# Moving one gate tanh and one weight split ahead of other ScalarE work, at the end of the token mixer's block loop

## The chip, the cores and the metric

The kernel runs on one core of one Trainium2 chip. The metric is the device time of one execution in microseconds (us), the median of several runs.

## The reference

The program is one layer of a hybrid backbone over 512 latent tokens of 1024 channels, with 256 context tokens as a prefix. The part that matters here is the end of the token mixer:

```python
glu_l, xr_l, gt_l, mg_l = jnp.split(hl @ w_in, SPLIT_IN, axis=-1)
...
y_a = _conformer_conv(glu, dw_conv, ln_conv_g, ln_conv_b, w_proj_conv)
y_b = (rec.astype(gt.dtype) * jax.nn.gelu(gt)) @ w_proj_lru
g_a, g_b = jnp.split(mg, 2, axis=-1)
return (jax.nn.sigmoid(g_a) * y_a + jax.nn.sigmoid(g_b) * y_b) @ w_out
```

`_conformer_conv` is a depthwise convolution of width 31 over the tokens, then a LayerNorm over the channels, a swish and a projection. After the mixer come a residual, a gated feed-forward part with a 3x3 depthwise convolution, and another residual; they are untouched here.

## The kernel before, in words

Channels lie on partitions, in eight blocks of 128, and tokens along the free axis. Every large product is float32 made of three fp32r matmuls (`mm3`, L133 to L136): each operand is kept as a high part and a low part, and high x high, high x low and low x high are summed in PSUM. A block of 128 output channels over 512 tokens takes 8 x 3 = 24 matmuls (`block`, L142).

Weights come in blocks of 512 KB through one list, in the order of use. `dma_to` (L97) issues the load of a block into a ring of three `raw` buffers from the SP queue. `cvt_to` (L108) splits it: ScalarE (ACT) rounds it into `whi` (L122), and GpSimd (POOL) subtracts that from the raw block into `wlo` (L123); both go to rings of four buffers. `W(key, look=2)` (L127) splits everything up to two blocks past the one asked for. At the place of the change the list is ga 0, ga 1, gb 0, gb 1, yb 0, gb 2, yb 1, gb 3, yb 2 and so on (L200 to L206): ga and gb are the columns of `w_in` for the two gates, yb those of `w_proj_lru`.

The schedule is written out by hand: each engine runs its instructions in the order of the code, and the tile framework adds the semaphore waits. The stretch concerned does this, in the order of the code:

- The block loop ends with the last scan (L655 to L658 on VectorE, DVE) and eight gelus (L674 on ACT).
- TensorE (PE) computes ga 0 and ga 1 (`ga_mm`, L775) into PSUM, while `gt_post` (L677) makes the input of the yb products: eight multiplications of gelu and scan on DVE (L679), eight roundings on ACT (L139, `rgh`), and eight subtractions (L140, `rgl`), six on DVE and those of blocks 2 and 5 on POOL.
- `ga_act` (L780) takes the tanh of a finished ga block from PSUM into the tile `sa` (L781). `sa` is a new tile in the space of the gelu buffers `ge` of the last blocks, so its first write comes after the last reads of those.
- `offload` (L559) does taps of the 31-wide convolution for channel blocks 6 and 7 on ACT (L565), and adds them up on POOL (L567).
- The loop at L793 runs over b = -1 to 7. It computes gb b+1 on PE, takes its tanh (`gate_act`, L384, tile `tg`), computes yb b, and joins both on DVE (`gate_mul`, L388). In between, `fill(n)` (L573) puts n instructions of the convolution on DVE (`conv31`, L525; L541).

PSUM for these products is two one-bank and two two-bank buffers, handed out by turns (`mm_any`, L80). ga 0, gb 0 and yb 0 follow one another on the two-bank pair, so yb 0 takes the buffer of ga 0, and yb 1 that of gb 0. ga 1, gb 1 and gb 2 follow on the one-bank pair, so gb 2 takes the buffer of ga 1.

When the convolution is through (`fill(1000)`, L830), POOL adds its last two blocks into `lnsum` (L553), and PE sums that over the channels into `mean` (L832). PE does these two matmuls between the two halves of ga 3; DVE then goes on with the LayerNorm (L839).

Of the kernel before, what the change touches and what calls it, by code (L numbers as in the profile page):

```python
# [37 lines left out]
def backbone_kernel(es: ExitStack, tc: tile.TileContext, x, ctxt, par, wadq, wada, win, wgate, wpc, wpl, wout,  # L38
# [20 lines left out]
    def col(name, i=0, n=None):  # L59
        o, w = _OFF[name]  # L60
        return P[:, o + i:o + (w if n is None else i + n)]
# [7 lines left out]
    def flat(t):  # L69
        return t.rearrange("p a b -> p (a b)") if len(t.shape) == 3 else t  # L70
# [9 lines left out]
    def mm_any(name):  # L80
        turn[0] += 1
        return mm1(name) if turn[0] % 2 else mm2(name)[:, 0:512]
# [8 lines left out]
    seq, index, raws, ready, pos = [], {}, {}, {}, {"dma": 0, "cvt": 0}  # L91
# [5 lines left out]
    def dma_to(i):  # L97
        while pos["dma"] < min(len(seq), i + 1):
            n = pos["dma"]
            src, shape = seq[n][:2]  # L100
            if n < 5:
                raws[n] = pq.tile([128] + shape, F32, tag="wa", bufs=10, name="raw")
            else:
                raws[n] = ring.tile([128] + shape, F32, tag="raw", bufs=3, name="raw")
            nc.sync.dma_start(out=raws[n], in_=src)
            pos["dma"] += 1

    def cvt_to(i):  # L108
        while pos["cvt"] < min(len(seq), i + 1):
            n = pos["cvt"]  # L110
            dma_to(n)
            _, shape, dst, raw, eng = seq[n]
            if raw:
                ready[n] = raws.pop(n)
            else:
                if dst is None:
                    hl = (ring.tile([128] + shape, F32R, tag="whi", bufs=4, name="whi"),
                          ring.tile([128] + shape, F32R, tag="wlo", bufs=4, name="wlo"))
                else:
                    hl = dst()  # L120
                t = raws.pop(n)
                S.activation(out=flat(hl[0]), in_=flat(t), func=AF.Copy)  # L122
                eng.tensor_sub(flat(hl[1]), flat(t), flat(hl[0]))  # L123
                ready[n] = hl
            pos["cvt"] += 1

    def W(key, look=2, ahead=2):  # L127
        i = index[key]
        cvt_to(i + look)
        dma_to(i + look + ahead)  # L130
        return ready[i]
# [10 lines left out]
    def block(ps, w, rh, rl, ks=range(NB)):  # L142
        hi, lo = w
        for k in ks:
            mm3(ps, hi[:, k, :], lo[:, k, :], rh[:, k, :], rl[:, k, :], k == 0, k == NB - 1)
# [236 lines left out]
    def gate_act(ps):  # L382
        t = t_tile("tg")
        S.activation(out=t, in_=ps, func=AF.Tanh, scale=0.5)  # L384
        return t

    def gate_mul(t, ps, dst):
        V.scalar_tensor_tensor(out=dst, in0=t, scalar=1.0, in1=ps, op0=ALU.add, op1=ALU.mult)  # L388
# [170 lines left out]
    def offload(n):  # L559
        for _ in range(min(n, 2 * n_off - off["k"])):  # L560
            k, b = 30 - off["k"] // 2, 6 + off["k"] % 2
            sc = col("dw31", 31 * b + k, 1)
            a = off["acc"][:, 512 * b - 3072:512 * b - 2560]
            o = a if k == 30 else off["prod"][:, 512 * b - 3072:512 * b - 2560]
            S.activation(out=o, in_=glu[:, b, k:k + T], func=AF.Copy, scale=sc)  # L565
            if k != 30:
                G.tensor_add(a, a, o)  # L567
            off["k"] += 1
# [4 lines left out]
    def fill(n):  # L573
        for _ in range(n):
            if not next(filler, False):
                return
# [100 lines left out]
    def gt_post(bs):  # L677
        for b in bs:
            V.tensor_mul(gts[b], gts[b], rec[:, b, :])  # L679
        for b in bs:  # L680
            split(gts[b], rgh[:, b, :], rgl[:, b, :], G if b % 3 == 2 else V)
# [98 lines left out]
    def ga_act(b):  # L780
        S.activation(out=sa[:, b, :], in_=gap[b][0], func=AF.Tanh, scale=0.5)  # L781
# [3 lines left out]
    ga_mm(1, look=1)  # L785
    cvt_to(index["gb", 1])
    gt_post(range(NB))
    cvt_to(index["yb", 0])
    yb = pd.tile([128, NB, T], F32, tag="d", name="yb")
    for b in (0, 1):  # L790
        ga_act(b)
    offload(4)
    for b in range(-1, NB):  # L793
        if b + 1 < NB:
            psg = mm_any("gb_ps")
            block(psg, W(("gb", b + 1)), Ahi, Alo)
            tn = gate_act(psg)
        if b < 0:
            t = tn
            continue  # L800
        fill(8 if b else 20)
        offload(2)
        ps = mm_any("yb_ps")
        block(ps, W(("yb", b)), rgh, rgl)
        gate_mul(t, ps, yb[:, b, :])
        t = tn
        fill(7)
        offload(2)
# [450 lines left out]
```

## Time and profile before

| what | value |
|---|---|
| median of 3 runs | 866.53 us (866.37 to 867.76) |
| profiled execution, its own time | 866.8 us |
| its span from first to last instruction | 865.0 us |
| PE busy | 848.0 us, 98% |
| DVE busy | 659.8 us, 76% |
| ACT busy | 431.5 us, 50% |
| POOL busy | 411.6 us, 48% |
| mean granted clock of PE | 0.998 of full speed |

A row of the timeline gives the start in us from the span's start, the length in us, the engine, the source line, the operation, the tile written and the tiles read; xN is a number of instructions merged into one row. In brackets at its end stands how long the engine was idle before it, and what ended that wait. Neighbouring instructions of an engine overlap a little, so a start can lie just ahead of the end of the one before.

### The profile page before, as it was taken

Reading aid. Unit: us, or ns where it says so; the run is one execution under the profiler, and the core shown is the slowest. Engines: PE = TensorE matmul, PEld = TensorE weight load, DVE = VectorE, ACT = ScalarE, POOL = GpSimd, SP = SyncE. Lnnn points to the kernel's source line nnn. Section 1 sums busy time; section 2 is a strip of 40 time slices with the busy share of each in tenths; the row PEclk is TensorE's granted clock in tenths of the full one; section 3 lists DMA queues with packets and bytes.
Section 4 is the critical chain, followed back from the end, with each engine's and each line's share of the span. In section 5 each row is a group of like instructions: output and inputs, shape, how many; then the busy total and the mean of one; then the engine's idle time right before and its main releaser. Section 6 shows DMA issues by size and latency. Waiting matters only on the chain.

```text
span 865.0 us, 11373 instructions
## 1 busy us (share of the span) xinstructions
PE 848.0 (98%) x4312; PEld 688.6 (80%) x4312; DVE 659.8 (76%) x932; ACT 431.5 (50%) x612; POOL 411.6 (48%) x227
## 2 busy tenths in 40 slices
PE   7999999999999999999999999999999999999997
PEld 6777888888877778877788889888888888888785
DVE  5355799999979999984555245999998989889204
ACT  5273777778777432226653255443443444345222
POOL 1234555566555565455332223355564456457820
PEclk9999999999999999999999999999999999999999
DMA  9952222222223232334843402314333333324402
GB/s 348 392 216 86 62 74 86 85 62 85 84 75 96 75 122 85 110 146 152 311 147 109 184 24 74 110 65 143 118 114 109 122 122 110 120 88 136 156 0 98
DMA packets 31398, 106.01 MB, mean 123 GB/s; under 512 B 3440, under 2 KB 3568, under 8 KB 31344
## 3 DMA queue, kind: packets, MB, share of 16 engines
q1 hardware_dynamic: 31344, 105.29, 35.0%
q8 instruction: 34, 0.56, 0.3%
q14 instruction: 20, 0.16, 0.1%
HBM read 103.17 MB, written 2.10 MB: 122 GB/s over the span
## 4 chain that ended last, share of the span: by engine, by line
PE 88%; DVE 6%; ACT 3%; issue 1%; DMA 1%; POOL 0%; SPq 0%; DVEq 0%; ACTq 0%; POOLq 0%
PE up_ps L135 9%; PE up_ps L134 9%; PE up_ps L136 9%; PE xr_ps L135 3%; PE xr_ps L136 3%; PE xr_ps L134 2%; PE ya_ps L134 2%; PE y_ps L134 2%; PE y_ps L135 2%; PE ya_ps L135 2%; PE ya_ps L136 2%; PE y_ps L136 2%; PE yb_ps L136 2%; PE yb_ps L135 2%; PE yb_ps L134 2%; PE g_ps L136 1%
## 5 line engine op out<-in xcount | busy, mean ns | idle before, releaser
L123 POOL TENSOR_TENSOR wlo<-raw,whi 128x1024 fp32r<-128x1024 f32 x117 | 290.0, 2491 | 223.1 <-ACT whi L122 216.7
L1053 DVE SCALAR_TENSOR_TENSOR cv<-zall,P,cv 128x512 f32<-128x512 f32 x240 | 161.8, 743 | 0.2
L541 DVE SCALAR_TENSOR_TENSOR cv<-glu,P,cv 128x512 f32<-128x512 f32 x228 | 153.2, 740 | 0.0
L122 ACT ACTIVATE whi<-raw 128x1024 fp32r<-128x1024 f32 x121 | 125.2, 1053 | 23.4 <-issue 11.0
L135 PE MATMUL up_ps<-Alo,whi 128*128 128x512 f32 (+1 forms) x352 | 132.7, 377 | 0.0
L134 PE MATMUL up_ps<-Ahi,whi 128*128 128x512 f32 (+1 forms) x352 | 132.0, 375 | 0.0
L136 PE MATMUL up_ps<-Ahi,wlo 128*128 128x512 f32 (+1 forms) x352 | 131.1, 372 | 0.0
L134 PEld LDWEIGHTS up_ps<-Ahi,whi 128*128 128x128 f32 x352 | 66.1, 188 | 13.7
L136 PEld LDWEIGHTS up_ps<-Ahi,wlo 128*128 128x128 f32 x352 | 66.2, 188 | 13.1
L135 PEld LDWEIGHTS up_ps<-Alo,whi 128*128 128x128 f32 x352 | 66.2, 188 | 12.6
L1039 POOL TENSOR_TENSOR acl<-fo,ach 128x512 fp32r<-128x512 f32 x20 | 26.0, 1300 | 85.6 <-ACT ach L1036 85.6
L1053 DVE SCALAR_TENSOR_TENSOR cv<-zall,P,cc 128x512 f32<-128x512 f32 x40 | 41.5, 1066 | 23.4 <-ACT cc L1027 23.4
L1025 ACT ACTIVATE zall<-up_ps 128x512 f32<-128x512 f32 x40 | 23.7, 593 | 63.4 <-PE up_ps L136 63.4
L1036 ACT ACTIVATE ach<-fo 128x512 fp32r<-128x512 f32 x20 | 12.7, 633 | 67.3 <-DVE fo L1035 67.3
L618 ACT ACTIVATE gate_ps<-gate_ps,P 128x768 f32<-128x768 f32 x32 | 28.0, 875 | 34.5 <-PE gate_ps L136 34.0
L384 ACT ACTIVATE tg<-gb_ps 128x512 f32<-128x512 f32 x8 | 4.8, 596 | 48.2 <-PE gb_ps L136 48.2
L1027 ACT ACTIVATE cc<-up_ps,P 128x512 f32<-128x512 f32 x40 | 27.3, 682 | 2.1 <-DVE cv L1053 2.1
L140 POOL TENSOR_TENSOR xl<-xc,xh 128x768 fp32r<-128x768 f32 x8 | 14.9, 1860 | 27.3 <-ACT xh L139 27.3
L1053 DVE SCALAR_TENSOR_TENSOR fo<-zall,P,cv 128x512 f32<-128x512 f32 x40 | 27.8, 734 | 0.0
L134 PE MATMUL yb_ps<-rgh,whi 128*128 128x512 f32 x64 | 25.4, 396 | 1.7 <-ACT sa L781 1.7
L136 PE MATMUL gb_ps<-Ahi,wlo 128*128 128x512 f32 x64 | 25.3, 395 | 1.0 <-POOL wlo L123 1.0
L134 PE MATMUL ga_ps<-Ahi,whi 128*128 128x512 f32 x64 | 26.0, 406 | 0.0
(387 smaller groups left out, 2114.7 us busy)
## 6 DMA issues: line engine op xcount, KB each, us to landing
raw<-in_win_dram SPq DMA_DIRECT2D x48, 512.0 KB, 3.3
raw<-in_wup_dram SPq DMA_DIRECT2D x40, 512.0 KB, 3.4
wa<-in_wada_dram SPq DMA_DIRECT2D x24, 512.0 KB, 6.0
raw<-in_wdn_dram SPq DMA_DIRECT2D x22, 512.0 KB, 3.3
wa<-in_wadq_dram SPq DMA_DIRECT2D x16, 512.0 KB, 9.2
raw<-in_wpl_dram SPq DMA_DIRECT2D x8, 512.0 KB, 3.3
raw<-in_wpc_dram SPq DMA_DIRECT2D x8, 512.0 KB, 5.0
raw<-in_wout_dram SPq DMA_DIRECT2D x8, 512.0 KB, 3.3
```

What stands on the lines that cost most here:

```text
L122: S.activation(out=flat(hl[0]), in_=flat(t), func=AF.Copy)
L123: eng.tensor_sub(flat(hl[1]), flat(t), flat(hl[0]))
L134: PE.matmul(o, lh, rh, start=first, stop=False)
L135: PE.matmul(o, lh, rl, start=False, stop=False)
L136: PE.matmul(o, ll, rh, start=False, stop=last)
L140: (eng or V).tensor_sub(lo, src, hi)
L541: V.scalar_tensor_tensor(out=cv[b] if k else glu[:, b, 0:T], in0=glu[:, b, k:k + T], scalar=col("dw31", 31 * b + k, 1), in1=cv[b], op0=ALU ...
L618: S.activation(out=lru[b, d, q], in_=lru[b, d, q], func=AF.Tanh, scale=0.5, bias=hb[:, i:i + 1])
L1025: S.activation(out=z[:, 1:1 + GH, 1:1 + GW], in_=ps.rearrange("p (r c) -> p r c", c=GW), func=AF.Copy)
L1027: S.activation(out=c, in_=ps.rearrange("p (r c) -> p r c", c=GW), func=AF.Copy, scale=col("dw9", 9 * (i + FW * (1 - s)) + 4, 1))
L1039: G.tensor_sub(acl[:, i, :], fo[i, 0], ach[:, i, :])
L1053: V.scalar_tensor_tensor(out=o, in0=zz[i, s][:, k // 3:k // 3 + GH, k % 3:k % 3 + GW], scalar=col("dw9", 9 * (i + FW * (1 - s)) + k, 1), i ...
```

## The change

```diff
     gt_post(range(NB))
-    cvt_to(index["yb", 0])
+    cvt_to(index["gb", 2])
     yb = pd.tile([128, NB, T], F32, tag="d", name="yb")
-    for b in (0, 1):
-        ga_act(b)
-    offload(4)
     for b in range(-1, NB):
         if b + 1 < NB:
             psg = mm_any("gb_ps")
...
             tn = gate_act(psg)
         if b < 0:
             t = tn
+            ga_act(0)
+            ga_act(1)
+            offload(4)
             continue
```

Ahead of the loop one weight block more is split, that of gb 2. The two ga tanh and the four offloaded taps now stand behind the first gb tanh, inside the loop. No instruction is added or removed. The order on PE, DVE and the SP queue is the same as before.

On ACT the place is the stretch between the roundings of `gt_post` (the x8 row) and the second gb tanh. `whi` is a weight block's rounding: of the two in the third and fourth row, the first is that of yb 0 and the added one that of gb 2.

```order
 L122 ACTIVATE whi<-raw 128x1024 x2
 L139 ACTIVATE rgh<-ge 128x512 x8
-L122 ACTIVATE whi<-raw 128x1024
+L122 ACTIVATE whi<-raw 128x1024 x2
+L384 ACTIVATE tg<-gb_ps 128x512
 L781 ACTIVATE sa<-ga_ps 128x512 x2
 L565 ACTIVATE off_acc<-glu,P 128x512 x2
 L565 ACTIVATE off_prod<-glu,P 128x512 x2
-L384 ACTIVATE tg<-gb_ps 128x512
-L122 ACTIVATE whi<-raw 128x1024
 L384 ACTIVATE tg<-gb_ps 128x512
 L122 ACTIVATE whi<-raw 128x1024 x2
```

The rounding of gb 2 and the tanh of gb 0 moved ahead of the two ga tanh and the four taps; the tanh of gb 1 now follows the taps directly.

On POOL the place is from the subtractions of `gt_post` (L140) to the first addition of the LayerNorm's sum (L546).

```order
 L123 TENSOR_TENSOR wlo<-raw,whi 128x1024 x5
 L140 TENSOR_TENSOR rgl<-ge,rgh 128x512 x2
-L123 TENSOR_TENSOR wlo<-raw,whi 128x1024
+L123 TENSOR_TENSOR wlo<-raw,whi 128x1024 x2
 L567 TENSOR_TENSOR off_acc<-off_acc,off_prod 128x512 x2
-L123 TENSOR_TENSOR wlo<-raw,whi 128x1024
 L546 TENSOR_TENSOR lnsum<-glu 128x512
 L123 TENSOR_TENSOR wlo<-raw,whi 128x1024 x7
```

The subtraction of gb 2 moved from behind the two additions of the taps to ahead of them, right behind the subtraction of yb 0.

## Rows read from the trace of the kernel before

**Rows 1.** The page, busy time of each engine: us, share, instructions.

```profile
PE 848.0 (98%) x4312; PEld 688.6 (80%) x4312; DVE 659.8 (76%) x932; ACT 431.5 (50%) x612; POOL 411.6 (48%) x227
```

**Rows 2.** Waits of PE from 300 to 865 us: total, times, longest.

```profile
PE yb_ps L134 <- ACT sa L781: 1.7, 1, 1.7
PE gb_ps L136 <- POOL wlo L123: 1.0, 1, 1.0
```

**Rows 3.** Windows: length; PE, PEld, DVE, ACT, POOL busy; granted clock; DMA share; GB/s.

```profile
296.00:304.00 8.00, 6.30 (x28) 4.80 (x27) 8.00 (x12) 4.59 (x8) 2.54 (x3) 1.00 0.22 66
308.00:388.00 80.00, 80.00 (x345) 64.34 (x344) 78.38 (x120) 17.80 (x21) 41.09 (x22) 1.00 0.37 125
```

**Rows 4.** Timeline of PE, the matmuls around its two waits, around mean, and the last.

```profile
297.97 0.39 PE L136 MATMUL gb_ps<-Ahi,wlo 128*128 128x512 f32 x1
300.06 0.50 PE L134 MATMUL yb_ps<-rgh,whi 128*128 128x512 f32 x1 [1.70 <-ACT sa L781]
...
305.98 0.39 PE L135 MATMUL gb_ps<-Alo,whi 128*128 128x512 f32 x1
307.36 0.50 PE L136 MATMUL gb_ps<-Ahi,wlo 128*128 128x512 f32 x1 [0.99 <-POOL wlo L123]
...
387.99 0.39 PE L136 MATMUL ga_ps<-Ahi,wlo 128*128 128x512 f32 x1
388.22 1.02 PE L832 MATMUL mean<-lnsum,ones 128*128 128x512 f32 x2
...
858.67 0.40 PE L136 MATMUL d2b<-whi,acl 128*128 128x512 f32 x1
```

**Rows 5.** Timeline of ACT: rounding of yb 0, ga tanh, rounding of gb 2.

```profile
292.94 1.04 ACT L122 ACTIVATE whi<-raw 128x1024 fp32r<-128x1024 f32 x1
299.41 1.09 ACT L781 ACTIVATE sa<-ga_ps 128x512 f32<-128x512 f32 x2 [5.43 <-DVE rgl L140]
...
303.31 1.06 ACT L122 ACTIVATE whi<-raw 128x1024 fp32r<-128x1024 f32 x1
```

**Rows 6.** Timeline of DVE: the last multiplications and subtractions, the convolution, the LayerNorm's start.

```profile
284.76 2.89 DVE L679 TENSOR_TENSOR ge<-ge,rec 128x512 f32<-128x512 f32 x1
...
294.60 2.89 DVE L140 TENSOR_TENSOR rgl<-ge,rgh 128x512 fp32r<-128x512 f32 x1
...
298.62 0.68 DVE L140 TENSOR_TENSOR rgl<-ge,rgh 128x512 fp32r<-128x512 f32 x1
...
303.83 8.64 DVE L541 SCALAR_TENSOR_TENSOR cv<-glu,P,cv 128x512 f32<-128x512 f32 x13
...
389.28 2.48 DVE L839 SCALAR_TENSOR_TENSOR glu<-mean,glu 128x512 f32<-128x512 f32 x4 [2.90 <-PE mean L832]
```

**Rows 7.** Timeline of POOL: weight subtractions (second of a pair, yb 0, gb 2), the last sums.

```profile
284.24 2.86 POOL L123 TENSOR_TENSOR wlo<-raw,whi 128x1024 fp32r<-128x1024 f32 x1
...
294.06 2.89 POOL L123 TENSOR_TENSOR wlo<-raw,whi 128x1024 fp32r<-128x1024 f32 x1 [0.53 <-ACT whi L122]
...
304.91 2.39 POOL L123 TENSOR_TENSOR wlo<-raw,whi 128x1024 fp32r<-128x1024 f32 x1
...
385.27 2.46 POOL L553 TENSOR_TENSOR lnsum<-lnsum,glu 128x512 f32<-128x512 f32 x2 [7.62 <-DVE glu L541]
```

**Rows 8.** Timeline of the SP queue: the issue of gb 2's raw block.

```profile
284.31 0.33 SPq L105 DMA_DIRECT2D raw<-in_win_dram  x1
```

**Rows 9.** DMA issues by line: count, KB each, median us to landing.

```profile
raw<-in_win_dram SPq DMA_DIRECT2D x48, 512.0 KB, 3.3
```

**Rows 10.** Windows of the program's end, columns as in rows 3.

```profile
858.00:862.00 4.00, 1.07 (x5) 0.54 (x3) 2.14 (x4) 0.98 (x3) 0.00 (x0) 0.96 0.00 0
862.00:865.00 3.00, 0.00 (x0) 0.00 (x0) 0.03 (x1) 0.00 (x0) 0.00 (x0) 0.50 0.45 175
```

**Rows 11.** Windows of L353's first matmuls alone: length; PE, PEld busy; clock; DMA; GB/s.

```profile
3.00:4.50 1.50, 1.50 (x9) 1.50 (x9) 1.00 1.01 347
4.90:6.40 1.50, 1.50 (x15) 1.50 (x15) 1.00 0.99 360
```

## The prediction

> **What bounds the kernel now.** I began with the busy times on the page: PE is busy 98% of the span [rows 1], so the time can only move where PE waits, or is made to wait. The view of waits names two waits of PE after 300 us and none later up to its last matmul [rows 2]: 1.7 us ahead of yb 0, for a ga tanh on ACT, and 1.0 us inside gb 2, for a weight subtraction on POOL. From there on PE runs without a gap [rows 3], so whatever PE loses or wins here arrives whole at the end, unless another wait takes it up before.
>
> The candidate for that is DVE. Between 308 and 388 us it is busy 78.38 of 80 us [rows 3], and the rest is its wait of 2.90 us for mean, of which 1.6 us lie inside the window [rows 6]. So the convolution ends when DVE's own work ends, whatever PE does. POOL's last sums follow and end at 385.27 + 2.46 = 387.73 us, and PE starts mean at 388.22, right behind a ga matmul [rows 4, 7]. The slack is 0.49 us: PE can come no more than about 0.4 us earlier here, and every us that DVE loses beyond it is lost for good.
>
> The next question is what releases the two waits. The ga tanh had waited 5.43 us for DVE's last subtraction of `gt_post` [rows 5], which ends at 298.62 + 0.68 = 299.30 [rows 6]; the tanh starts at 299.41, and yb 0 at 300.06. So this wait is not made by ACT's order. The wait in gb 2 is: its rounding ran only at 303.31 and its subtraction at 304.91 to 307.30, against PE at 307.36 [rows 4, 5, 7].
>
> **The change part by part.**
>
> *The wait in gb 2 goes.* Its raw block is issued at 284.31 and takes 3.3 us to land [rows 8, 9]. Its rounding can follow that of yb 0 at about 293.9 (292.94 + 1.04) [rows 5], and its subtraction on POOL that of yb 0, at 296.9 (294.06 + 2.89) [rows 7]. Both are done some 7 us ahead of PE. At PE's pace of 0.233 us the matmul that started at 307.36 was due at 306.21, and its own length of 0.50 in place of 0.39 delays the next by 0.11 [rows 4]: the gain on PE is 1.15 + 0.11 = 1.26 us.
>
> *The tanh order costs nothing by itself.* The tanh of gb 0 reads a block done well before 297.97 + 0.39, and needs no `sa`. The ga tanh still wait for DVE's last subtraction. The tanh of gb 1 follows the taps directly, and is wanted only when PE reuses its buffer, after yb 0 and gb 2, more than 10 us later. SP and PE keep their orders.
>
> *The moved subtraction meets DVE's subtractions.* This is the term that decides. Before, POOL was free from 296.95 to 302.40 (5.46 us ahead of the taps' additions), while DVE did its last three subtractions; now POOL subtracts gb 2 there. What two such instructions do to each other is in the trace. A DVE subtraction that starts alone takes 0.68 us. One that starts while POOL subtracts a weight block takes 2.89, and ends 0.54 after POOL's: the one at 294.60 ends at 297.49, POOL's at 296.95 [rows 6, 7]. Where POOL has two weight subtractions in a row, DVE gets one instruction in between and is then held again: POOL's second at 284.24 takes 2.86 (2.39 alone), and the DVE multiplication started at 284.76 takes 2.89 and ends 0.55 after it. That is the pattern of the change: yb 0's subtraction holds DVE's third until 297.49, then gb 2's (296.9 to about 299.76) holds the fourth, from 297.42 to about 300.3. The cost to DVE is 2.89 - 0.68 = 2.21 us. No time comes back where gb 2's subtraction used to be: there DVE ran convolution steps, 13 in 8.64 us, undisturbed by POOL [rows 6, 7].
>
> So the last subtraction ends at 301.51, the ga tanh starts at 301.62, and yb 0 at 302.27. DVE, which has no idle time to give, carries the 2.21 us to the end of the convolution: POOL's last sums end at 389.94 and mean can start at 390.00 (0.06 after, like PE behind POOL in gb 2).
>
> *PE's idle time, and its clock.* Behind the last matmul ahead of yb 0 (297.97 + 0.39 = 298.36) PE now idles until 302.27, 3.9 us in place of 1.7. With 1.7 the granted clock stayed at 1.00 [rows 3]. The one other end of a busy stretch in the trace is the last: PE's final matmul ends at 858.67 + 0.40 = 859.07 [rows 4], and the granted clock is 0.96 on average over 858 to 862 and 0.50 after it [rows 10]. That makes 0.3 us at half clock before 862, so it fell near 861.7, after 2.6 us of idleness. 3.9 us is on the far side of that, so I take the fall as the likelier case. PE then starts yb 0 at 1.2 GHz. The price comes from the program's start, by the matmuls' pace (the clock column has no lower value there): 9 in 1.5 us before 4.5 us, 15 in 1.5 us from 4.9 [rows 11]. Started at 1.50, they took 3.0 to 3.4 us to reach the high pace. At half pace such a stretch loses 1.5 to 1.7 us; I take 1.6. The bounds are nothing (the clock stays, as at 1.7 us of idleness) and twice that (two such stretches, if the first counts for too little).
>
> The Trainium skill, in "TensorE: Matmul & The Clock Gate", section "What's actually happening", says that the low clock is the default and that activity releases it, so that idleness brings it back. By that rule the fall would come and the sum is the higher one below; if the wait of 1.7 us is the measure, it would not, and the sum is the lower one. The trace of before holds both behaviours, and no wait of 3.9 us between.
>
> **Sum.** PE's arrival at mean: + 2.21 (yb 0 later) - 1.26 (gb 2) + 1.6 (clock) = + 2.55 us, so 390.77; the sums were ready at 390.00, so nothing is added there. PE is gapless after it, hence + 2.55 at the end: 866.8 + 2.55 = 869.35 against the profiled execution. The median of the runs lies 0.27 below that execution, so the forecast is **869.1 us**.
>
> **The rivals.**
>
> *The clock stays up.* PE would reach mean at 388.22 + 0.95 = 389.17 and wait for the sums until 390.00, with a slower start of 0.11: + 1.89, or 868.4 us. For it: no wait of PE in the middle of this kernel has ever cost the clock. Against it: the tail fell after less.
>
> *DVE keeps its place, and the kernel is not slower.* If POOL's subtraction of gb 2 waits until DVE has done all six of its own, the splits end at 299.30 as before and only the gain at gb 2 is left. It decides at 297.4 us: whichever has started there, POOL's (due at 296.9) or DVE's fourth, holds the other. PE would then come to mean 1.26 us earlier, but the sums end at 387.73, so it starts at 387.79, with 0.11 for the restart: 0.32 us less, 866.2 us. For it: at 294.0 a DVE subtraction did get ahead, since POOL waited there for ACT until 294.06 [rows 7]. Against it: POOL's next instruction is ready here, its rounding being done at about 295, and the pair at 284.24 shows who wins then. The Trainium skill says the same in "SBUF — State Buffer", section "Who interferes with whom": a VectorE instruction with two SBUF inputs contends with a GpSimd one that reads SBUF, and the one issued first blocks the other. By that, this rival would need gb 2's rounding to be late.
>
> *Two stretches at half clock.* + 2.55 + 1.6 = + 4.15, or 870.7 us, if the first stretch holds too much idleness for the clock to come back.
>
> **How the numbers follow.** Forecast 0.52, clock stays up 0.30, DVE keeps its place 0.10, two stretches 0.08. The forecast's own spread is 868.5 to 869.4 (1.0 to 1.7 us for the clock, as the fall may come before PE starts again, and some 0.2 on the 2.21). With the case of the clock staying up, and the scatter of a median on both, the range is 867.5 to 869.9; it leaves out the two small cases. What a measurement of this kernel can tell from no change is about 0.2%, 1.7 us, so up to 868.3. The forecast lies above that nearly whole (0.49 of its 0.52), the case at 868.4 about half (0.15), the last case whole: slower 0.72. Faster needs 1.7 us off, and the sums cap every gain at 0.4: 0.03, for what I have not seen. The rest, 0.25, is the same.
>
> **What would show it.** In the profile after: gb 2's subtraction on POOL near 296.9; one more DVE subtraction of 2.9 us, and the last ending near 301.5; the ga tanh near 301.6; PE's wait ahead of yb 0 at 3.9 us in place of 1.7, and none in gb 2; a granted clock below 1.00 between 300 and 308, and the first matmuls of yb 0 about twice 0.233 us apart; POOL's last sums ending near 389.9. I am wrong if all DVE subtractions after 297 us take 0.68, or if a wait ahead of mean swallows more or less than I say; if the clock stays at 1.00 the 1.6 us go, and a wait of about 0.8 us ahead of mean takes the place of part of them.

## The result, and the profile after

The changed kernel takes 873.13 us (median of 5 runs, 871.75 to 874.52) against 866.53 for the kernel before. The medians lie 6.6 us apart; the ratio that comes with a 95% interval is 1.0069 (1.0056 to 1.0082), or 6.0 us. Either way the time is outside the range of 867.5 to 869.9. The sign was forecast, the size was not, and the loss does not sit where it was put. The profiled execution took 871.75 us, with a span of 870.0 us against 865.0; it is the shortest of the five, so its rows explain 5 us of the loss.

The waits of PE from 282 to 440 us (total, times, longest) look quite different from [rows 2]:

```profile
PE mean L832 <- POOL lnsum L553: 6.1, 1, 6.1
PE yb_ps L136 <- POOL wlo L123: 0.6, 1, 0.6
PE ada_cp L310 <- DMA wa<-in_wada_dram: 0.2, 1, 0.2
```

Both waits of before are gone, the one ahead of yb 0 included. One of 6.1 us has appeared ahead of mean, and a small one of 0.6 us in yb 1. PE's timeline at the two places (start, length; it answers to [rows 4]):

```profile
297.49 0.39 PE L136 MATMUL gb_ps<-Ahi,wlo 128*128 128x512 f32 x1
297.72 0.39 PE L134 MATMUL yb_ps<-rgh,whi 128*128 128x512 f32 x1
...
385.13 0.39 PE L136 MATMUL ga_ps<-Ahi,wlo 128*128 128x512 f32 x1
391.61 2.08 PE L832 MATMUL mean<-lnsum,ones 128*128 128x512 f32 x2 [6.08 <-POOL lnsum L553]
```

yb 0 follows gb 1 at PE's pace of 0.23 us, at 297.72. The ga tanh run only at 301.09, as ACT's timeline shows (it answers to [rows 5]; the first row holds the roundings of yb 0 and gb 2):

```profile
292.43 2.00 ACT L122 ACTIVATE whi<-raw 128x1024 fp32r<-128x1024 f32 x2
294.33 0.57 ACT L384 ACTIVATE tg<-gb_ps 128x512 f32<-128x512 f32 x1
301.09 1.09 ACT L781 ACTIVATE sa<-ga_ps 128x512 f32<-128x512 f32 x2 [6.19 <-DVE rgl L140]
```

So yb 0 no longer depends on them. DVE's timeline answers to [rows 6]; everything in this execution starts 0.5 us earlier than in the one before (the first subtraction at 291.78 in place of 292.29):

```profile
291.78 9.22 DVE L140 TENSOR_TENSOR rgl<-ge,rgh 128x512 fp32r<-128x512 f32 x6
...
347.42 3.55 DVE L533 SCALAR_TENSOR_TENSOR cv<-glu,P,off_acc 128x512 f32<-128x512 f32 x2
...
393.72 2.48 DVE L839 SCALAR_TENSOR_TENSOR glu<-mean,glu 128x512 f32<-128x512 f32 x4 [3.49 <-PE mean L832]
```

The six subtractions took 7.01 us together before and take 9.22 now: the hold of 2.21 us that was forecast (a hold, here and below, is the time by which an instruction of one of these two engines is longer while one of the other runs). But there is a second one. The two steps that start the convolution of blocks 6 and 7 (L533, the only ones that add `off_acc`, which lies in SBUF like their other input) took 1.41 us before, and take 3.55 now. The same stretch before, DVE and then POOL:

```profile
345.72 1.41 DVE L533 SCALAR_TENSOR_TENSOR cv<-glu,P,off_acc 128x512 f32<-128x512 f32 x2
```

```profile
348.03 2.40 POOL L123 TENSOR_TENSOR wlo<-raw,whi 128x1024 fp32r<-128x1024 f32 x1 [4.00 <-ACT whi L122]
```

There DVE was through when POOL's weight subtractions came. POOL's timeline after (it answers to [rows 7]; the first row holds yb 0 and gb 2):

```profile
293.55 5.69 POOL L123 TENSOR_TENSOR wlo<-raw,whi 128x1024 fp32r<-128x1024 f32 x2 [0.54 <-ACT whi L122]
...
345.18 5.24 POOL L123 TENSOR_TENSOR wlo<-raw,whi 128x1024 fp32r<-128x1024 f32 x2 [4.02 <-ACT whi L122]
...
389.12 2.43 POOL L553 TENSOR_TENSOR lnsum<-lnsum,glu 128x512 f32<-128x512 f32 x2 [14.33 <-DVE glu L541]
```

PE is ahead, so POOL's pair comes at 345.18 in place of 348.03; DVE is behind, so L533 comes at 347.42 in place of 345.72, and now they meet. POOL's last sums end at 389.12 + 2.43 = 391.55, 3.8 us later than before, or 4.3 with the 0.5 us of the earlier start: the two holds of 2.21 and 2.14. The windows around mean, columns as in [rows 3], show what the wait brings with it:

```profile
388.00:391.00 3.00, 0.00 (x0) 0.00 (x0) 2.23 (x4) 0.00 (x0) 1.80 (x2) 0.50 0.00 0
391.00:393.00 2.00, 1.39 (x3) 0.84 (x3) 0.00 (x0) 0.00 (x0) 2.00 (x2) 0.50 0.00 0
393.00:395.00 2.00, 2.00 (x6) 1.25 (x5) 1.28 (x3) 0.56 (x1) 2.00 (x2) 0.64 0.17 16
395.00:397.00 2.00, 2.00 (x11) 1.59 (x10) 1.90 (x5) 1.95 (x5) 1.28 (x2) 1.00 0.67 246
```

The granted clock falls to 0.50, the 1.2 GHz level, while PE waits, and is back at 1.00 only near 394.4 (0.64 over 393 to 395 makes 1.4 us at 0.50). From 391.6 to 394.4 PE works 2.8 us at half pace and loses 1.4. The sum for this execution: the sums 4.3 us later, less 0.4 of slack that they had, 1.4 for the clock, 0.2 for a later DMA wait of PE, less the earlier start of 0.5: 5.0 us, the difference of the spans.

### The profile page after: what moved, and what is told of

The parts are those of the page before. It is cut to its first block, busy times and chain, and to the rows that moved or that the text cites. A ratio compares the mean times of both kernels' runs of the same rounds, so it can differ in the third digit from the quotient of the medians.

```text
span 870.0 us, 11374 instructions
## 1 busy us (share of the span) xinstructions
PE 849.6 (98%) x4312; PEld 689.6 (79%) x4312; DVE 663.2 (76%) x932; ACT 431.4 (50%) x612; POOL 412.2 (47%) x227
## 4 chain that ended last, share of the span: by engine, by line
PE 76%; DVE 15%; DMA 3%; issue 2%; ACT 2%; POOL 1%; SPq 0%; DVEq 0%; POOLq 0%; ACTq 0%
DVE cv L541 9%; PE up_ps L135 9%; PE up_ps L134 9%; PE up_ps L136 9%; PE xr_ps L136 2%; PE xr_ps L135 2%; PE xr_ps L134 2%; PE ya_ps L134 2%; PE y_ps L134 2%; PE ya_ps L136 2%; PE ya_ps L135 2%; PE y_ps L135 2%; PE y_ps L136 2%; DMA raw<-in_win_dram 1%; PE g_ps L134 1%
## 5 line engine op out<-in xcount | busy, mean ns | idle before, releaser
L541 DVE SCALAR_TENSOR_TENSOR cv<-glu,P,cv 128x512 f32<-128x512 f32 x228 | 153.3, 742 | 0.0
L140 POOL TENSOR_TENSOR xl<-xc,xh 128x768 fp32r<-128x768 f32 x8 | 14.9, 1859 | 27.3 <-ACT xh L139 27.3
L136 PE MATMUL yb_ps<-rgh,wlo 128*128 128x512 f32 x64 | 25.4, 397 | 0.6 <-POOL wlo L123 0.6
L136 PE MATMUL gt_ps<-Ahi,wlo 128*128 128x512 f32 x64 | 25.4, 397 | 0.3 <-POOL wlo L123 0.3
L134 PE MATMUL ya_ps<-slh,whi 128*128 128x512 f32 x64 | 25.6, 400 | 0.0
```

The lines of the kernel that those rows point to most:

```text
L134: PE.matmul(o, lh, rh, start=first, stop=False)
L136: PE.matmul(o, ll, rh, start=False, stop=last)
L140: (eng or V).tensor_sub(lo, src, hi)
L541: V.scalar_tensor_tensor(out=cv[b] if k else glu[:, b, 0:T], in0=glu[:, b, k:k + T], scalar=col("dw31", 31 * b + k, 1), in1=cv[b], op0=ALU ...
```

## The experiments

From the profile after I formed **theory A**: moving the tanh of gb 0 ahead frees PE (3 us), the early split holds DVE, the shifted timing of POOL and DVE holds it again at L533, and PE, which waits for DVE's result at mean, can only turn its lead into idle time. **Theory D**: that idle time also costs the clock. Ratios are to runs of the kernel before on the same chip, with 95% intervals.

**The tanh order alone** (the split stays where it was):

```diff
-    cvt_to(index["gb", 2])
+    cvt_to(index["yb", 0])
```

> Only the two ga tanh and the four taps move behind the first gb tanh; the split of gb 2 stays where it was. Theory A (a PSUM buffer goes to the next tile in the order in which its readers release it, and the order of the tanh decides that): yb 0 takes the buffer of gb 0 and starts without a wait, about 1.9 us earlier than before; gb 2 then waits some 3 us for its own late weight split, so that PE goes on at about 307.4 us as before; no DVE subtraction after 297 us is held (0.68 us each); POOL's last sums end as before, at 387.7. Time 866.5 us if the clock holds through the wait of 3 us, up to 868.2 if it falls. Rival B (the buffers rotate, and yb 0 lost its wait through the earlier weight split): yb 0 still waits 1.7 us, nothing else changes, 866.5 us.

Measured: 868.82 us, ratio 1.0021 (1.0012 to 1.0031). PE has one wait from 282 to 440 us, and yb 0 follows gb 1 without a gap:

```profile
PE gb_ps L136 <- POOL wlo L123: 2.6, 1, 2.6
```

The six subtractions take 7.02 us, as before. The time is 0.6 us above the upper value expected. The clock falls after this wait of 2.6 us:

```profile
310.00:313.00 3.00, 3.00 (x9) 2.32 (x8) 3.00 (x6) 0.00 (x0) 3.00 (x2) 0.50 0.44 141
```

PE does 9 matmuls in these 3 us, where 13 are its pace. So the order of the tanh alone frees yb 0, which rival B denied, and the lead is lost in gb 2. Of the 2.3 us by which this trace's span is longer than before, 1.0 lies ahead of the change (the first subtraction of `gt_post` starts at 293.33 in place of 292.29); the other 1.3 come behind the wait, where the clock is low.

**The split alone** (the kernel before, with gb 2 split early):

```diff
-    cvt_to(index["yb", 0])
+    cvt_to(index["gb", 2])
```

> Only the weight split of gb 2 moves ahead of the ga tanh; tanh and taps stay where they were. Theory A: yb 0 takes the buffer of ga 0, as in the kernel before, and now waits 3.9 us for the ga tanh, which waits for a DVE subtraction that is held once, for 2.2 us; the second hold (of the convolution step that reads off_acc) does not come, since POOL's pair is about 1 us late there and not early; POOL's last sums end near 389.9; 868.4 us if the clock holds, 869.1 if it falls: the case that was predicted for the whole change. Rival B (the early split frees yb 0): no wait ahead of yb 0, and the time is that of the whole change, 872 to 874 us.

Measured: 869.93 us, ratio 1.0031 (1.0019 to 1.0043). PE's wait, the subtractions of DVE, and the window behind the wait:

```profile
PE yb_ps L134 <- ACT sa L781: 3.8, 1, 3.8
```

```profile
292.11 9.18 DVE L140 TENSOR_TENSOR rgl<-ge,rgh 128x512 fp32r<-128x512 f32 x6
```

```profile
302.00:304.00 2.00, 1.97 (x5) 1.58 (x6) 2.00 (x4) 2.00 (x4) 0.00 (x0) 0.50 0.11 45
```

One hold, a wait of 3.8 us at yb 0, half clock behind it, and L533 at 1.41 us: this is what the prediction described, at + 0.31% where it had worked out + 2.55 us, 0.29%. For this half of the change its mechanism was right; the median lies 0.8 us above the 869.1 of the expectation, and the profiled execution, 868.90, is the shortest of the five.

**DVE's work reordered, first attempt** (four convolution steps while POOL subtracts gb 2):

```diff
             split(gts[b], rgh[:, b, :], rgl[:, b, :], G if b % 3 == 2 else V)
+            if b == 3:
+                fill(4)
```

> The changed kernel, with four steps of the convolution put between DVE's third and fourth subtraction, where POOL now subtracts gb 2; DVE does the same work in another order. Theory A (DVE is held twice, once for each of two separate meetings with POOL): the first hold is gone (all subtractions after the third take 0.68 us), the convolution is level with the kernel before until 345 us, and there one of the two steps that read off_acc is still held for about 2.2 us by POOL's pair; POOL's last sums end near 389.9, PE waits for them some 4.5 to 5 us, and the time is 868.5 to 870.5 us. Rival C (one hold explains the loss, the rest is the clock): nothing is left of the loss, POOL's last sums end at 387.7 and the time is at or below 867 us.

Measured: 872.96 us, ratio 1.0071 (1.0059 to 1.0083): outside both expectations. Both holds are gone in its trace, and POOL's last sums end at 387.50. But the convolution now ends four steps earlier in the code, so these sums stand ahead of a weight subtraction of ga on POOL's queue, and PE waits for that:

```profile
PE ga_ps L136 <- POOL wlo L123: 5.9, 1, 5.9
```

It says nothing for or against the second hold, nor on rival C. It does show how a change in DVE's order reaches PE through POOL's.

**The same, with POOL's order kept**:

```diff
+            if b == 3:
+                fill(4)
...
-        fill(8 if b else 20)
+        fill(8 if b else 16)
```

> As the run with four steps put between DVE's third and fourth subtraction, but these four are taken from the 20 ahead of the first join, so that from there on DVE's and POOL's orders are those of the changed kernel (in the earlier run the convolution ended four steps early in the code, and POOL's last sums came ahead of a weight subtraction of ga 3, for which PE then waited 5.9 us). Theory A: the first hold is gone, and DVE is level with the kernel before when it comes to the two steps that read off_acc, within 0.1 us of POOL's pair; whichever of them POOL gets ahead of is held for about 2.2 us. If one is, POOL's last sums end near 389.9, PE waits 4 to 5 us, 868.5 to 870.5 us; if none is, they end near 387.7, PE waits 2.3 to 2.8 us, 866 to 868 us. Rival C (the first hold is the whole loss): no wait ahead of mean of over 1 us, 864.5 us or less.

Measured: 868.66 us (866.01 to 870.92), ratio 1.0006 (0.9991 to 1.0020). In its profiled execution neither hold occurs, and PE's wait at mean is 1.3 us:

```profile
302.58 1.89 DVE L140 TENSOR_TENSOR rgl<-ge,rgh 128x512 fp32r<-128x512 f32 x3
...
348.24 1.42 DVE L533 SCALAR_TENSOR_TENSOR cv<-glu,P,off_acc 128x512 f32<-128x512 f32 x2
```

Of its twelve runs five lie at 866.0 to 866.7, one at 867.9 and six at 869.4 to 870.9. The lower ones fit the case of no hold, level with the lowest runs of the kernel before on that chip (866.2 to 866.9). What the upper ones had was not seen, but for the profiled one of 869.44, which lost its time at the program's start (last section). I had worked out a wait of 2.3 to 2.8 us; it is shorter since PE also waited 1.0 us in yb 1. Rival C falls: the wait ahead of mean is there with neither hold, and no run came to 864.5.

**DVE ahead of both meetings.** Seven steps of the convolution go between DVE's second and third subtraction, where POOL subtracts yb 0 and gb 2:

```diff
-            split(gts[b], rgh[:, b, :], rgl[:, b, :], G if b % 3 == 2 else V)
+            S.activation(out=rgh[:, b, :], in_=gts[b], func=AF.Copy)
+        for b in (2, 5):
+            G.tensor_sub(rgl[:, b, :], gts[b], rgh[:, b, :])
+        cvt_to(index["gb", 2])
+        for b in (0, 1, 3, 4, 6, 7):
+            V.tensor_sub(rgl[:, b, :], gts[b], rgh[:, b, :])
+            if b == 1:
+                fill(7)
...
-        fill(8 if b else 20)
+        fill(8 if b else 13)
```

> The changed kernel, with seven steps of the convolution taken from the 20 ahead of the first join of the loop (13 are left there) and put between DVE's second and third subtraction, so that DVE does them while POOL subtracts yb 0 and gb 2; the roundings and POOL's subtractions are issued in the same order as in the changed kernel. Theory A (the change gives PE about 3 us, and DVE's meetings with POOL take them away): no DVE subtraction from the second on is held; DVE is about 2 us ahead of the kernel before, passes the two steps that read off_acc ahead of POOL's pair, and POOL's last sums end near 385.5; PE waits under 1 us for them, the clock holds; 863.2 to 864.6 us. Rival F (PE's lead would be lost later whatever DVE does): 866 us or more, with a wait of PE of over 2 us that is not the one ahead of mean.

Measured: 865.29 us, ratio 0.9982 (0.9969 to 0.9994). PE's wait for the sums is down to 0.4 us, with 0.3 us in yb 1 and 0.5 us for a DMA. Theory A holds in its main point and rival F falls: with the holds of 2.2 us gone, the same change gains. The time is 0.7 us above what theory A expected, and the next run's rows show one reason, a third and shorter hold. The seven steps were not tried in the kernel before; there yb 0 waits for DVE's last subtraction, which they would delay, so a gain from them alone is unlikely but not excluded by a run.

**The same, and all of ga 3 ahead of mean**:

```diff
-        ga_mm(b, range(NB if b < 3 else 4))
+        ga_mm(b)
...
-    ga_mm(3, range(4, NB))
```

> As the run before, and all 24 matmuls of ga 3 stand ahead of mean in place of 12, which gives PE 2.8 us more to do before it needs POOL's sums. Theory A: no wait ahead of mean, the clock holds; 863.0 to 864.2 us, at most 0.8 less than the run before. Rival G (PE runs out of work behind mean, since the LayerNorm's sums are ready only some 10 us after it): a wait ahead of var of up to 1.5 us, and no gain against the run before.

Measured: **864.38 us, ratio 0.9962 (0.9948 to 0.9977)**, 2.5 us better than the kernel before by the medians and the lowest median of the study, though its interval overlaps that of the run before. It is 0.2 us above the expectation. From 282 us to the end PE has one wait:

```profile
PE yb_ps L136 <- POOL wlo L123: 0.3, 1, 0.3
```

The holds of 2.2 us are gone from DVE's last four subtractions, but not every hold: four without one would take 2.5 us, and these take 3.39. The second of them starts while POOL does its first addition of the LayerNorm's sum (L546, 1.10 us in the changed kernel), which now comes this early, and takes 1.58 us in place of 0.68:

```profile
299.19 3.39 DVE L686 TENSOR_TENSOR rgl<-ge,rgh 128x512 fp32r<-128x512 f32 x4
299.79 1.58 DVE L686 TENSOR_TENSOR rgl<-ge,rgh 128x512 fp32r<-128x512 f32 x1
```

```profile
299.25 1.56 POOL L546 TENSOR_TENSOR lnsum<-glu 128x512 f32<-128x512 f32 x1
```

That is 0.9 us, and POOL's last sums end at 386.41, 0.9 us later than the 385.5 worked out for the run before. Mean comes behind a ga matmul again, at 388.69:

```profile
383.94 2.47 POOL L553 TENSOR_TENSOR lnsum<-lnsum,glu 128x512 f32<-128x512 f32 x2 [8.63 <-DVE glu L541]
```

Mean is no earlier than before (388.22), but PE has done 12 matmuls more by then, and does not miss them behind it: no wait ahead of var, so rival G falls.

**Small matmuls during the wait, 54 and then 20**, into the PSUM tile of ga 4, in the changed kernel:

```diff
+    ps4 = mm_any("ga_ps")
+    warm(ps4, 54)
     mean, acc4 = cv_tile("mean"), cv_tile("ada_cp")
...
-    ga_mm(4, look=1)
+    gap[4] = ps4, W(("ga", 4), 1)
+    ga_mm(4)
```

> The changed kernel, with 54 small matmuls of ones (into the PSUM tile of ga 4, overwritten later) ahead of mean, so that PE is busy during most of its wait for POOL's last sums. Theory D (the half clock after that wait costs real time): the granted clock stays at 1.00 past mean; mean starts at the same time; 1.0 to 2.5 us less than the changed kernel, 870.5 to 872 us. Rival E (the clock costs nothing there, DVE's path alone sets the time): 872 to 874 us as in the changed kernel.

Measured with 54: 878.34 us, ratio 1.0131 (1.0118 to 1.0145). I had counted one pass of 0.11 us for each of these matmuls; a float32 one is two rows in the trace, so they ran to 397.5, far past the sums (389.51), and the time tells nothing on the clock. Its trace does show something else. Up to 385 us it is the program of the changed kernel, and here L533 was not held; POOL was:

```profile
347.52 1.41 DVE L533 SCALAR_TENSOR_TENSOR cv<-glu,P,off_acc 128x512 f32<-128x512 f32 x2
```

```profile
345.20 5.99 POOL L123 TENSOR_TENSOR wlo<-raw,whi 128x1024 fp32r<-128x1024 f32 x2 [3.98 <-ACT whi L122]
```

POOL's last sums then end at 389.51, 2.0 us earlier than in the changed kernel. L533 starts at 347.52 here and at 347.42 in the changed kernel, with POOL's pair at 345.20 and 345.18. So the second hold is decided by who comes first, within about 0.1 us, and differs between executions.

> As the run with 54 small matmuls ahead of mean, but with 20: each is two passes in the trace of about 0.113 us, so that they fill 4.5 of the 6.1 us. Theory D (the half clock after the wait costs real time): granted clock 1.00 past mean, mean starts as in the changed kernel, 1.0 to 2.5 us less than it: 870.5 to 872 us. Rival E (the clock costs nothing there): 872 to 874 us.

Measured with 20: 871.68 us, ratio 1.0041 (1.0027 to 1.0055). Its profiled execution, with both holds, took 870.06 us. Mean starts at 391.53, as in the changed kernel (391.61), and the clock stays up:

```profile
388.00:391.00 3.00, 1.91 (x18) 1.72 (x16) 2.14 (x4) 0.00 (x0) 1.89 (x2) 1.00 0.00 0
391.00:394.00 3.00, 2.47 (x9) 1.72 (x10) 1.31 (x3) 0.58 (x1) 3.00 (x3) 1.00 0.00 0
```

1.7 us less than the profiled changed kernel, with useless work in PE's wait: theory D holds, rival E falls. Of the 1.7 us, 0.1 is the earlier mean and 0.2 a DMA wait that did not come; the clock's 1.4 is the rest.

**The changed kernel with all of ga 3 ahead of mean** (the edit of the best version alone):

> The changed kernel, with all 24 matmuls of ga 3 ahead of mean in place of 12, nothing else. Theory A: POOL's last sums end as in the changed kernel, PE's wait for them shrinks from 6.1 to about 3.3 us, and since 2.8 us of PE's work lie ahead of it, the time is 2.8 us less: 869 to 870.5 us, the clock still falling. Rival G (behind mean, PE now waits for the LayerNorm's sums): 871.5 us or more, with a new wait ahead of var.

Measured: 870.19 us, ratio 1.0028 (1.0017 to 1.0039), 2.9 less than the changed kernel. PE's wait shrinks as expected, and the clock still falls:

```profile
PE mean L832 <- POOL lnsum L553: 3.3, 1, 3.3
```

```profile
394.00:400.00 6.00, 6.00 (x16) 4.18 (x15) 4.46 (x8) 3.66 (x7) 5.12 (x3) 0.59 0.27 87
```

**The taps later, on top of the best version** (without the four taps behind the ga tanh):

```diff
             ga_act(1)
-            offload(4)
```

> As the run with seven steps moved and ga 3 whole ahead of mean, and the four taps no longer stand together behind the ga tanh: two are done at each of the two next places of the loop that ask for them, so that the weight subtraction of yb 1 comes ahead of the taps' additions on POOL. Theory A: the 0.3 us that PE waits in yb 1 for that subtraction go; 863.7 to 864.4 us, not to be told from the run before. Rival (the later taps delay the tanh or the roundings that PE waits for): a new wait of PE near 305 to 325 us, 865 us or more.

Measured: 865.10 us, ratio 0.9969 (0.9957 to 0.9981). PE has no wait between 282 and 440 us, so the rival's new wait did not come, but the time is 0.7 us above theory A's expectation and cannot be told from that of the best version (0.9962).

## Why the prediction was wrong

**What held.** PE bound the kernel, its only two waits behind 300 us were those named, and a lead of PE beyond 0.4 us was worth nothing ahead of mean. The hold of DVE came at the place and with the price forecast (2.21 us forecast and measured), and gb 2 lost its wait. The price of the half clock was near in size (1.6 forecast; 1.4 in the changed kernel, 1.5 at yb 0 with the split alone), its place was not. It had been read from matmuls whose clock column shows 1.00 [rows 11]; that their slow pace was half clock was a guess. The price is no constant either: with all of ga 3 ahead of mean, PE worked at half clock from 393.2 to 398.9, which costs 2.8 us. The sign was no luck: DVE's delay alone, beyond the 0.4 us of slack, makes the kernel slower.

**The step that failed** is "The tanh order costs nothing by itself", with the sentence it rests on, "the ga tanh still wait for DVE's last subtraction ... So the last subtraction ends at 301.51, the ga tanh starts at 301.62, and yb 0 at 302.27". The two ga tanh did start late; yb 0 did not wait for them. I took the two-bank buffers to rotate, so that yb 0 must have that of ga 0. Before, it had. Now the tanh of gb 0 stands ahead of those of ga in the code, and yb 0 starts with the ga tanh still to come. The two halves alone show that the order of the tanh does this (a wait of 3.8 us with the old order, none with the new). There are two two-bank buffers, and that of ga 0 is still to be read, so yb 0 has that of gb 0. That the pool hands out buffers in the order in which their readers release them fits all these traces; it is inferred, since no row names a buffer's address.

**What followed from it.** PE gained about 1.9 us at yb 0 where I had it lose 2.2, so its last matmul ahead of mean starts 2.9 us earlier in the trace (385.13 against 387.99), 2.4 without the earlier start, not 2.55 later. It stands idle from 385.53 (391.61 - 6.08). I had a wait ahead of mean of 0 or 0.8 us; it is 6.1. The clock fell there, as it would have at yb 0.

**The term that was mis-sized** is DVE's delay: 2.21 us forecast, 4.3 measured. The second hold, of L533, was not foreseen. I wrote that no time comes back at the convolution since its steps ran "undisturbed by POOL", and asked no further whether one of them might lose some. Undisturbed is right for L541, which has one input in PSUM, and not for L533, whose inputs are both in SBUF. It had run free before only because POOL's pair came 2.3 us later.

Of the rivals, none had yb 0 free. The Trainium skill's rule in "SBUF — State Buffer", section "Who interferes with whom", would have found the second hold: it names VectorE instructions with two SBUF inputs. The trace agrees with it here, in L140 and L533. I had checked the convolution by its commonest row alone. The trace also agrees with what the Trainium skill says in "TensorE: Matmul & The Clock Gate", section "What's actually happening", that idleness brings the low clock back (0.50 in the wait of 6.1 us).

The 1.4 us between the profiled execution and the median was not traced. When the clock comes back (2.8 us of PE's work at half pace here, 5.7 with all of ga 3 ahead of mean) and how late the program's start leaves the change (up to 3.3 us, last section) both differ between executions; which of them made the runs of 873 and 874.5 us stays open.

## What to carry to other kernels

Where one engine makes the result that the bounding engine needs next, a lead won upstream becomes idle time; first find work to put into it, or make the late engine faster. Moving a GpSimd instruction that reads SBUF is a change to VectorE too: list VectorE's instructions with two SBUF inputs at the new place and at every place whose phase shifts, not only the nearest. And which buffer a tile takes can change with the order in which the readers of earlier tiles stand in the code, so a wait for a buffer has to be derived anew for the changed order.

## What the hardware showed that I had not expected

The clock falls sooner than the waits of before suggested: in the changed kernel some 2.1 us after PE's last matmul ended (385.52 to about 387.6), 2.2 us with all of ga 3 ahead of mean, and with the tanh order alone at about 309.8, 1.5 us after PE had taken up work again behind a wait of 2.6. It is not always so soon: with the split alone it fell 3.4 us after PE's last matmul (298.18 to about 301.5). Waits of 1.3 and 1.6 us ahead of mean did not bring it down. It also falls in some executions near the program's start, where PE waits for its first inputs. In the run with four steps moved and POOL's order kept it was at 0.50 early on (windows, columns as in [rows 3]):

```profile
12.00:14.00 2.00, 1.61 (x10) 1.07 (x7) 1.96 (x5) 0.00 (x0) 0.00 (x0) 0.50 1.01 404
14.00:20.00 6.00, 6.00 (x68) 4.35 (x66) 1.57 (x3) 1.55 (x3) 0.33 (x2) 0.64 1.02 408
```

Its first subtraction of `gt_post` then starts at 294.83 in place of 292.29, so 2.5 us were gone before the change came into play. The code up to there is the same in all kernels, so this is no effect of any edit, and part of why single runs of one kernel lie up to 4 us apart. The profiled executions with seven steps moved (0.51 over 14 to 20 us) and of the tanh order alone (0.81) were 3.3 and 1.0 us late in the same way. Two traces are to be compared only after the difference of their starts is taken off.
